# Neighbourhood attention: a unit's weighted values in one row, behind all of its copies

## The chip, the cores and the metric

One core of a Trainium2 chip runs the whole program in one launch. The metric is the device time of that core in microseconds. The engines are named as in the profile: PE (TensorE, matmuls and transpositions, with PEld for its weight loads), DVE (VectorE), ACT (ScalarE), POOL (GpSimd), SP (SyncE, which issues most DMAs).

## The reference, cut to what matters

Two blocks follow each other on 1024 tokens of width 1024. The first has a dilated attention layer and an S5 state-space layer; the second has two hybrid layers, each with a short convolution, a retention and a neighbourhood attention side by side, one output projection and a layer norm. The change concerns the neighbourhood attention (six heads of 64, a grid of 16 rows by 64 columns, a window of 8 by 16, and 256 context tokens that every query sees too) and, by a shared helper, the dilated attention.

```python
def row_block(args):
    ...
    s_loc = jnp.einsum('bhcd,bhrckd->bhcrk', q_r, k_win).astype(F32) * scale
    ...
    s_ctx = jnp.einsum('bhcd,bhjd->bhcj', q_r, kch).astype(F32) * scale
    p = jax.nn.softmax(jnp.concatenate([s_loc.reshape(b, NA_HEADS, GRID_W, n_loc), s_ctx], axis=-1), axis=-1)
    ...
    return (jnp.einsum('bhcrk,bhrckd->bhcd', p_loc, v_win)
            + jnp.einsum('bhcj,bhjd->bhcd', p_ctx, vch))
```

All of it is float32, and the kernel keeps that precision. The projections take three matmuls on rounded high and low halves (mm<-aTh,wh, mm<-aTl,wh, mm<-aTh,wl); the weighted values are plain float32 matmuls, each of which leaves two records in the trace.

## The kernel before

In a hybrid layer the neighbourhood attention goes by three pairs of heads (na_project(p), then na_core(p)). For one pair, na_core lists small functions: transpositions of the values, then units (rt, m), two halves of the grid (rt) by four column blocks (m), so 8 units for a pair, 24 for a layer and 48 in all. A unit has three steps, and step s1 of unit i, s2 of unit i-1 and s3 of unit i-2 are written together.

- **s1**: scores S of 128 queries for two heads a: 256 context keys (one PSUM tile for both heads) and 384 grid keys (a tile for each head), each product in two float32 parts. Then `soft`: DVE adds the bias and takes the maximum (L1789, L1793), and ACT takes the exponential of all 640 columns into nsb (L1796).
- **s2**: for each head four transpositions of 128 columns into a PSUM tile T (L1826), and the fifth, of the last 128 of the 640 keys, into a tile tx that both heads share (L1827). Head 0's tile is copied to nPT by DVE (L1830), head 1's by ACT (L1832), and tx to nPX by ACT (L1835). The tag T has two PSUM buffers, S three, O one; nPT has three, nPX two.
- **s3**: ten matmuls, five blocks of keys by two heads. Each puts 64 columns of V in the array and makes 64 rows of the output O; the two heads go to the two column halves. The blocks are written in the order 4, 0, 1, 2, 3, so nPX is used first, then nPT. After the last unit of a half, `put` weighs O with the gate and sends it to DRAM (yd).

The helper `together` (L128) takes these ten: it issues the first, and the others only under `issue_after(first)`, so that none comes ahead of the first. The dilated attention's s3 (L492) uses the same helper for a group of four blocks (up to 16 matmuls with V), whose copies PT are made in its s2 by DVE (L488) and ACT (L489); three other calls are in the S5 layer.

What is written around the units are projections of the next pair (mm, L168). They run `tick` now and then, which takes the next small function. The final order on each engine isn't the written one: the program is built with a scheduler that simulates a timeline and picks for each engine the ready instruction of highest priority; a priority falls with the place in the program. So the ten matmuls of a unit can come apart where something else is ready earlier.

At a layer's end, the output projection reads yd back through two slabs (ys, fetched by ACT's queue, L1974 and L1975), splits them into a high and a low half (ACT L1978, DVE L1979) and multiplies with the split output weights wo (PE L168); out_ln takes the product from PSUM (L2041).

Of the kernel before, what the change touches and what calls it, by code (L numbers as in the profile page):

```python
# [75 lines left out]
class Ker:  # L76
# [51 lines left out]
    def together(self, todo):  # L128

        mm = self.nc.tensor.matmul  # L130
        (o, w, m, a, z), *rest = todo
        first = mm(o, w, m, start=a, stop=z)  # L132
        with self.tc.issue_after(first.ins):
            for o, w, m, a, z in rest:
                mm(o, w, m, start=a, stop=z)  # L135
# [104 lines left out]
    def attn(self, zs):  # L240
# [11 lines left out]
        with ExitStack() as es:  # L252
# [194 lines left out]
            def steps(p, g, T, bt, st, O):  # L447
# [32 lines left out]
                def s2(n):  # L480
# [7 lines left out]
                    nc.vector.tensor_copy(PT[:, 0:N], t[:, 0:N])  # L488
                    nc.scalar.activation(PT[:, 256:256 + N], t[:, 256:256 + N], AF.Copy)  # L489
                    live[n] = (first, PT)  # L490

                def s3(m):  # L492

                    o = self.ps.tile([128, 512], F32, tag="O", name=self.uid("O"), bufs=1)
                    todo = []
                    for n in (4 * m + 3, 4 * m, 4 * m + 1, 4 * m + 2):
                        first, PT = live.pop(n)
# [7 lines left out]
                    self.together(todo)  # L505
# [825 lines left out]
    def hybrid(self, l, need_ctx, x_src, x_dst, xc_src=None, xc_dst=None):  # L1331
# [13 lines left out]
        with ExitStack() as es:  # L1345
# [378 lines left out]
            with ExitStack() as ns:  # L1724
# [25 lines left out]
                def na_core(p):  # L1750
# [68 lines left out]
                    def s2(rt, m):  # L1819
                        P = L.pop(("P", rt, m))  # L1820
                        out = []
                        tx = self.pt()
                        for a in range(2):
                            t = self.pt()
                            for b in range(4):
                                nc.tensor.transpose(t[:, b * 128:b * 128 + 128], P[a][:, b * 128:b * 128 + 128], self.ident)  # L1826
                            nc.tensor.transpose(tx[:, a * 128:a * 128 + 128], P[a][:, 512:640], self.ident)  # L1827
                            o = wp.tile([128, 512], F32, tag="nPT", name=self.uid("nPT"), bufs=3)
                            if a == 0:
                                V.tensor_copy(o, t)  # L1830
                            else:
                                ACT.activation(o, t, AF.Copy)  # L1832
                            out.append(o)
                        o = wp.tile([128, 256], F32, tag="nPX", name=self.uid("nPX"), bufs=2)
                        ACT.activation(o, tx[:, :256], AF.Copy)  # L1835
                        L["PT", rt, m] = (out, o)

                    def s3(rt, m):
                        PT, px = L.pop(("PT", rt, m))
# [5 lines left out]
                        for b in (4, 0, 1, 2, 3):  # L1845
                            for a in range(2):
# [4 lines left out]
                                todo.append((t, v, pp, b == 4, b == 3))  # L1851
                        self.together(todo)
# [289 lines left out]
```

## Time and profile before

| | before |
|---|---|
| median of 3 runs | 3177.37 us (3173.4 to 3179.25) |
| the profiled execution, time and span | 3182.18 us, 3180.2 us |
| PE busy | 3089.3 us, 97% |
| DVE, ACT, POOL busy | 1906.7, 1192.0, 598.4 us |
| mean granted clock of PE | 0.992 |

PE is the engine to look at. The dilated attention runs from some 350 to 1166 us, the neighbourhood units of layer 1 from 2117 to 2390 and of layer 2 from 2850 to 3081. In the profile a matmul's own duration includes the time in which the next one is already streaming, so what one costs is read from the start of one to the start of the next. Rows of equal neighbours are merged with a count.

### The profile page before, as it was taken

The page shows a single profiled execution, that of the slowest core. Times are in us where ns is not written, and L with a number is a line of the kernel's source. Part 1 is how long each engine was busy: PE and PEld are TensorE (multiplying, and loading weights), DVE is VectorE, ACT ScalarE, POOL GpSimd, SP SyncE. Part 2 cuts the span into 40 slices and gives each one's busy share as a digit, 9 for nine tenths or more (in the row PEclk, how much of TensorE's full clock was granted, in tenths as well). Part 3 has the DMA queues.
Part 4 walks back from the last instruction along what each step waited for, and adds up shares of the span by engine and source line. Part 5 has one row for each costly group of instructions (what it writes and reads, how often), then busy time and mean ns, then how long its engine had stood idle before and what let it go on. Part 6 is the DMA issues. An engine that isn't in the chain of part 4 may idle for free. (4 is left out here: it accounts for less than half of the span.)

```text
span 3180.2 us, 47784 instructions
## 1 busy us (share of the span) xinstructions
PE 3089.3 (97%) x18100; PEld 2541.0 (80%) x18100; DVE 1906.7 (60%) x4099; ACT 1192.0 (37%) x2492; POOL 598.4 (19%) x769
## 2 busy tenths in 40 slices
PE   8999999999999999999999999999999999999998
PEld 6777878777877887787878888788887888888877
DVE  4676676677666657655654634455557754465565
ACT  4222555555554544322431112244342212234351
POOL 0365120222111201111003122310002212220001
PEclk9999999999999999999999999999999999999999
DMA  5455232333233235565342211121125321121132
GB/s 199 151 184 175 68 101 82 88 108 89 82 95 88 82 103 178 172 183 158 124 145 88 80 42 59 49 81 57 48 72 161 109 67 57 57 74 58 51 118 93
DMA packets 331226, 324.05 MB, mean 102 GB/s; under 512 B 28697, under 2 KB 272116, under 8 KB 330996
## 3 DMA queue, kind: packets, MB, share of 16 engines
q1 hardware_dynamic: 322644, 312.75, 32.0%
q10 hardware_dynamic: 8352, 8.26, 0.8%
q8 instruction: 142, 2.33, 0.3%
q14 instruction: 88, 0.72, 0.1%
HBM read 248.27 MB, written 72.67 MB: 101 GB/s over the span
## 5 line engine op out<-in xcount | busy, mean ns | idle before, releaser
L168 PE MATMUL mm<-aTh,wh 128*128 128x512 f32 x2304 | 918.9, 399 | 12.4 <-ACT yr L639 3.6
L168 PE MATMUL mm<-aTl,wh 128*128 128x512 f32 x2304 | 915.8, 398 | 0.2 <-DVE aTl L1072 0.2
L168 PE MATMUL mm<-aTh,wl 128*128 128x512 f32 x2304 | 915.2, 397 | 0.6 <-DVE wl L155 0.6
L168 PEld LDWEIGHTS mm<-aTh,wh 128*128 128x128 f32 x2304 | 436.4, 189 | 104.8 <-issue 4.9
L168 PEld LDWEIGHTS mm<-aTh,wl 128*128 128x128 f32 x2304 | 435.9, 189 | 86.8 <-issue 2.4
L168 PEld LDWEIGHTS mm<-aTl,wh 128*128 128x128 f32 x2304 | 436.2, 189 | 84.7 <-issue 2.7
L155 DVE TENSOR_TENSOR wl<-wr,wh 128x1024 fp32r<-128x1024 f32 x158 | 200.3, 1268 | 209.5 <-ACT wh L154 208.2
L154 ACT ACTIVATE wh<-wr 128x1024 fp32r<-128x1024 f32 x158 | 166.9, 1057 | 336.5 <-PE mm L168 286.6
L475 ACT ACTIVATE sb<-sb,st 128x128 f32<-128x128 f32 (+1 forms) x384 | 170.1, 444 | 257.7 <-DVE st L473 256.1
L168 PE MATMUL mm<-wo,aTh 128*128 128x512 f32 x768 | 243.5, 399 | 9.8 <-DVE ys L2041 4.9
L1205 DVE SCALAR_TENSOR_TENSOR ma<-mw,cact,ma 128x256 f32<-128x256 f32 x336 | 182.9, 548 | 19.4 <-DMA mw<-in_w_mod 13.3
L168 PEld LDWEIGHTS mm<-wo,aTh 128*128 128x128 f32 x768 | 144.5, 191 | 41.7 <-DVE hs L1154 4.5
L168 PE MATMUL mm<-wo,aTl 128*128 128x512 f32 x384 | 151.8, 395 | 0.5 <-DVE aTl L1979 0.4
L473 DVE CUSTOM_DVE_ANT_0 sb<-S,bt 128x128 f32<-128x128 f32 (+1 forms) x384 | 125.0, 344 | 45.4 <-PE T L486 29.5
L427 POOL CAST qk<-kz 64x512 fp32r<-64x512 f32 x64 | 65.5, 1023 | 359.8 <-ACT kz L421 342.1
L1796 ACT ACTIVATE nsb<-nsb,nmn 128x640 f32<-128x640 f32 (+1 forms) x108 | 85.7, 793 | 99.3 <-DVE nmn L1793 84.6
L486 PE MATMUL T<-ident,sb 128*128 128x128 f32 x560 | 105.1, 284 | 13.2 <-ACT PT L489 4.1
L168 PE MATMUL mm<-vh,aTl 128*128 128x512 f32 x288 | 114.7, 398 | 0.0
L168 PE MATMUL mm<-vh,aTh 128*128 128x512 f32 x288 | 114.1, 396 | 0.0
L168 PE MATMUL mm<-vl,aTh 128*128 128x512 f32 x288 | 113.6, 395 | 0.0
L168 PE MATMUL mm<-cTh,wl 128*128 128x256 f32 x352 | 100.8, 286 | 0.6 <-DVE wl L155 0.6
L168 PE MATMUL mm<-cTh,wh 128*128 128x256 f32 x352 | 101.3, 288 | 0.0
(448 smaller groups left out, 5685.6 us busy)
## 6 DMA issues: line engine op xcount, KB each, us to landing
wr<-in_attn_w_in SPq DMA_DIRECT2D x80, 512.0 KB
wr<-in_w_in SPq DMA_DIRECT2D x64, 512.0 KB
mw<-in_w_mod SPq DMA_DIRECT2D x48, 512.0 KB
vd<-vo SPq DMA_DIRECT2D x48, 256.0 KB
Wb<-wgd SPq DMA_DIRECT2D x96, 128.0 KB
x<-x SPq DMA_DIRECT2D x24, 512.0 KB
x<-in_x SPq DMA_DIRECT2D x16, 512.0 KB
V<-vd SPq DMA_DIRECT2D x32, 256.0 KB
```

Source lines behind the costliest of these rows:

```text
L154: nc.scalar.activation(h, raw, AF.Copy)
L155: nc.vector.tensor_tensor(l, raw, h.bitcast(F32), op=ALU.subtract)
L168: nc.tensor.matmul(out, s_, m_, start=first and i == 0, stop=last and i == len(todo) - 1)
L427: nc.gpsimd.tensor_copy(at(t[o], g, hf), at(h_[r], g, hf))
L473: nc.vector.tensor_tensor_reduce(out=sb[:, :N], in0=sp[:, a * 256:a * 256 + N], in1=b, scale=1.0, scalar=3e38, op0=ALU.add, op1=ALU.min, a ...
L475: nc.scalar.activation(sb[:, :N], sb[:, :N], AF.Exp, bias=mc, scale=-1.0, accum_out=st[:, 1, g, a, n:n + 1])
L486: nc.tensor.transpose(t[:, c:c + 128], Ps[a][:, b * 128:b * 128 + 128], self.ident)
L1205: V.scalar_tensor_tensor(a, L[h][:, k], c, a, op0=ALU.mult, op1=ALU.add)
L1796: ACT.activation(sb[:, :n], sb[:, :n], AF.Exp, bias=mc, scale=-1.0, accum_out=den)
```

## The change

No instruction is added, removed or resized. Three things move.

1. `together` gets a list `made`. The first matmul waits for every instruction in it. The others are issued with a priority raised by 4000, for every caller of the helper.
2. In the neighbourhoods, the two transpositions into tx come behind the eight others (they are issued after the last of them), and all three copies go into `made`. The blocks are taken in the order 4, 3, 2, 1, 0 and the heads as 1, 0.
3. In the dilated attention the two copies of each of a group's four blocks go into `made`; the order of its matmuls stays.

```diff
@@ -125,12 +125,16 @@
         while self.bg:
             self.bg.popleft()()
 
-    def together(self, todo):
+    def together(self, todo, made=()):
+
 
         mm = self.nc.tensor.matmul
         (o, w, m, a, z), *rest = todo
         first = mm(o, w, m, start=a, stop=z)
-        with self.tc.issue_after(first.ins):
+        for i in made:
+            self.tc.add_manual_dep(first.ins, i.ins.name, mybir.DependencyInfo(
+                mybir.DependencyClass.Sync, mybir.DependencyReason.DATA), reason="together")
+        with self.tc.high_priority(4000), self.tc.issue_after(first.ins):
             for o, w, m, a, z in rest:
                 mm(o, w, m, start=a, stop=z)
 
@@ -485,16 +489,17 @@
                             c = a * 256 + b * 128
                             nc.tensor.transpose(t[:, c:c + 128], Ps[a][:, b * 128:b * 128 + 128], self.ident)
                     PT = ap.tile([128, 512], F32, tag="PT", name=self.uid("PT"), bufs=5)
-                    nc.vector.tensor_copy(PT[:, 0:N], t[:, 0:N])
-                    nc.scalar.activation(PT[:, 256:256 + N], t[:, 256:256 + N], AF.Copy)
-                    live[n] = (first, PT)
+                    made = [nc.vector.tensor_copy(PT[:, 0:N], t[:, 0:N]),
+                            nc.scalar.activation(PT[:, 256:256 + N], t[:, 256:256 + N], AF.Copy)]
+                    live[n] = (first, PT, made)
 
                 def s3(m):
 
                     o = self.ps.tile([128, 512], F32, tag="O", name=self.uid("O"), bufs=1)
-                    todo = []
+                    todo, made = [], []
                     for n in (4 * m + 3, 4 * m, 4 * m + 1, 4 * m + 2):
-                        first, PT = live.pop(n)
+                        first, PT, by = live.pop(n)
+                        made += by
                         blocks = [n] if first else [n - 1, n]
                         for b, kb in enumerate(blocks):
                             for a in (1, 0):
@@ -502,7 +507,7 @@
                                              V[:, kb, 64 * a:64 * a + 64],
                                              PT[:, a * 256 + b * 128:a * 256 + b * 128 + 128],
                                              b == 0, b == len(blocks) - 1))
-                    self.together(todo)
+                    self.together(todo, made)
                     ov = O[:, m * 512:m * 512 + 512].rearrange("p (n i) -> p n i", i=128)
                     nc.vector.tensor_copy(ov, o.rearrange("p (n i) -> p n i", i=128)[:, :, ::-1])
 
@@ -1818,38 +1823,39 @@
 
                     def s2(rt, m):
                         P = L.pop(("P", rt, m))
-                        out = []
+                        out, made = [], []
                         tx = self.pt()
                         for a in range(2):
                             t = self.pt()
                             for b in range(4):
-                                nc.tensor.transpose(t[:, b * 128:b * 128 + 128], P[a][:, b * 128:b * 128 + 128], self.ident)
-                            nc.tensor.transpose(tx[:, a * 128:a * 128 + 128], P[a][:, 512:640], self.ident)
+                                z = nc.tensor.transpose(t[:, b * 128:b * 128 + 128], P[a][:, b * 128:b * 128 + 128],
+                                                        self.ident)
                             o = wp.tile([128, 512], F32, tag="nPT", name=self.uid("nPT"), bufs=3)
-                            if a == 0:
-                                V.tensor_copy(o, t)
-                            else:
-                                ACT.activation(o, t, AF.Copy)
+                            made.append(V.tensor_copy(o, t) if a == 0 else ACT.activation(o, t, AF.Copy))
                             out.append(o)
+
                         o = wp.tile([128, 256], F32, tag="nPX", name=self.uid("nPX"), bufs=2)
-                        ACT.activation(o, tx[:, :256], AF.Copy)
-                        L["PT", rt, m] = (out, o)
+                        with self.tc.issue_after(z.ins):
+                            for a in range(2):
+                                nc.tensor.transpose(tx[:, a * 128:a * 128 + 128], P[a][:, 512:640], self.ident)
+                        made.append(ACT.activation(o, tx[:, :256], AF.Copy))
+                        L["PT", rt, m] = (out, o, made)
 
                     def s3(rt, m):
-                        PT, px = L.pop(("PT", rt, m))
+                        PT, px, made = L.pop(("PT", rt, m))
                         if m == 0:
                             L["o"] = self.ps.tile([128, 512], F32, tag="O", name=self.uid("O"), bufs=1)
                             L["sto"] = L["st"]
                         o = L["o"]
                         todo = []
-                        for b in (4, 0, 1, 2, 3):
-                            for a in range(2):
+                        for b in (4, 3, 2, 1, 0):
+                            for a in (1, 0):
                                 e = slice(a * 64, a * 64 + 64)
                                 t = o[e, m * 128:m * 128 + 128]
                                 v = Vc[:, b, e] if b < 2 else Vt[:, (rt + b - 2) * 4 + m, e]
                                 pp = PT[a][:, b * 128:b * 128 + 128] if b < 4 else px[:, a * 128:a * 128 + 128]
-                                todo.append((t, v, pp, b == 4, b == 3))
-                        self.together(todo)
+                                todo.append((t, v, pp, b == 4, b == 0))
+                        self.together(todo, made)
                         if m == 3:
                             put(o, weigh(L["sto"][:, :8].rearrange("p (m a) -> p m a", a=2),
                                          384 + p * 128, rt * 512, 4), rt)
```

How the order on PE moves is shown at three places. In each row stand the line, the operation, out<-in and the shape.

The first is the first unit of layer 1. Before, on PE (O is the output, nPX and nPT the transposed probabilities, mm a projection):

```order
L1813 MATMUL S_19557<-nk_19163,nqq_19266 128x384
L1813 MATMUL S_19557<-nkz_16703,nqq_19266 128x384
L132 MATMUL O_19595<-nPX_19545,nV_19376 64x128
L135 MATMUL O_19595<-nPX_19545,nV_19376 64x128
L135 MATMUL O_19595<-nPT_19535,nVc_19377 64x128
L168 MATMUL mm_19734<-aTh,wh_19378 128x512
L168 MATMUL mm_19734<-aTl,wh_19378 128x512
```

Seven more matmuls of this unit follow before's rows, in runs of six and one, behind eight projections. After, on PE:

```order
L172 MATMUL mm_19734<-aTl,wh_19378 128x512
L133 MATMUL O_19595<-nPX_19543,nV_19376 64x128
L139 MATMUL O_19595<-nPX_19543,nV_19376 64x128
L139 MATMUL O_19595<-nPT_19541,nV_19376 64x128
L139 MATMUL O_19595<-nPT_19534,nV_19376 64x128
L139 MATMUL O_19595<-nPT_19541,nV_19376 64x128
L139 MATMUL O_19595<-nPT_19534,nV_19376 64x128
L139 MATMUL O_19595<-nPT_19541,nVc_19377 64x128
L139 MATMUL O_19595<-nPT_19534,nVc_19377 64x128
L139 MATMUL O_19595<-nPT_19541,nVc_19377 64x128
L139 MATMUL O_19595<-nPT_19534,nVc_19377 64x128
L1818 MATMUL S_19556<-nk_19162,nqq_19265 128x384
```

The unit's ten stand in one row, with grid scores S ahead of them before and behind them now.

The second place is the end of a stretch with few projections, in layer 2. Before, on PE, the last unit of a half (T are transpositions, of the same tile nsb by L1827 into tx):

```order
L132 MATMUL O_26182<-nPX_26239,nV_25710 64x128
L135 MATMUL O_26182<-nPX_26239,nV_25710 64x128
L135 MATMUL O_26182<-nPT_26229,nVc_25711 64x128
L1826 MATMUL T_26252<-ident,nsb_26212 128x128 x4
L1827 MATMUL T_26251<-ident,nsb_26212 128x128
L135 MATMUL O_26182<-nPT_26237,nVc_25711 64x128
L135 MATMUL O_26182<-nPT_26229,nVc_25711 64x128
L135 MATMUL O_26182<-nPT_26237,nVc_25711 64x128
L135 MATMUL O_26182<-nPT_26229,nV_25710 64x128
L135 MATMUL O_26182<-nPT_26237,nV_25710 64x128
L135 MATMUL O_26182<-nPT_26229,nV_25710 64x128
L135 MATMUL O_26182<-nPT_26237,nV_25710 64x128
```

After, on PE:

```order
L1840 MATMUL T_26222<-ident,nsb_26153 128x128
L1840 MATMUL T_26222<-ident,nsb_26158 128x128
L1831 MATMUL T_26252<-ident,nsb_26212 128x128 x4
L133 MATMUL O_26182<-nPX_26237,nV_25710 64x128
L139 MATMUL O_26182<-nPX_26237,nV_25710 64x128
L139 MATMUL O_26182<-nPT_26235,nV_25710 64x128
L139 MATMUL O_26182<-nPT_26228,nV_25710 64x128
L139 MATMUL O_26182<-nPT_26235,nV_25710 64x128
L139 MATMUL O_26182<-nPT_26228,nV_25710 64x128
L139 MATMUL O_26182<-nPT_26235,nVc_25711 64x128
L139 MATMUL O_26182<-nPT_26228,nVc_25711 64x128
L139 MATMUL O_26182<-nPT_26235,nVc_25711 64x128
```

Before, a run of three and one of seven with five transpositions between; now ten, of which the last stands just behind, and the transpositions of the unit's last keys moved to a place that is four transpositions ahead of its first value.

The third is the end of layer 2's neighbourhoods. Before, on PE (wo are output weights, aTh and aTl the halves of their input):

```order
L168 MATMUL mm_28112<-wo_27969,aTh 128x512
L168 MATMUL mm_28112<-wo_27970,aTh 128x512
L168 MATMUL mm_28112<-wo_27969,aTl 128x512
L135 MATMUL O_27775<-nPT_27859,nVc_27317 64x128
L135 MATMUL O_27775<-nPT_27851,nVc_27317 64x128
L135 MATMUL O_27775<-nPT_27859,nVc_27317 64x128
L135 MATMUL O_27775<-nPT_27851,nV_27316 64x128
L135 MATMUL O_27775<-nPT_27859,nV_27316 64x128
L135 MATMUL O_27775<-nPT_27851,nV_27316 64x128
L135 MATMUL O_27775<-nPT_27859,nV_27316 64x128
L168 MATMUL mm_28138<-wo_27969,aTh 128x512
L168 MATMUL mm_28138<-wo_27970,aTh 128x512
```

After, on PE:

```order
L139 MATMUL O_27775<-nPT_27857,nVc_27317 64x128
L139 MATMUL O_27775<-nPT_27850,nVc_27317 64x128
L139 MATMUL O_27775<-nPT_27857,nVc_27317 64x128
L139 MATMUL O_27775<-nPT_27850,nVc_27317 64x128
L1873 MATMUL T_27897<-ident,non_27893 128x128 x4
L172 MATMUL mm_28112<-wo_27993,aTh 128x512
L172 MATMUL mm_28138<-wo_27993,aTh 128x512
L172 MATMUL mm_28112<-wo_27993,aTh 128x512
L172 MATMUL mm_28112<-wo_27993,aTl 128x512
L172 MATMUL mm_28112<-wo_27998,aTh 128x512
L172 MATMUL mm_28138<-wo_27993,aTh 128x512
L172 MATMUL mm_28138<-wo_27993,aTl 128x512
```

Three output matmuls stood ahead of the last run and the others behind it; now 18 of them stand ahead of this unit's first value, and behind its last come four transpositions for the gate and then the rest.

## Rows read from the trace of the kernel before

**Rows 1.** Part 1 of the page: busy us (share of span) xinstructions.

```profile
PE 3089.3 (97%) x18100; PEld 2541.0 (80%) x18100; DVE 1906.7 (60%) x4099; ACT 1192.0 (37%) x2492; POOL 598.4 (19%) x769
```

**Rows 2.** Windows, neighbourhood stretches: length, PE, PEld, DVE, ACT, POOL busy, granted clock, DMA share, GB/s.

```profile
2110.00:2190.00 80.00, 80.00 (x558) 65.51 (x557) 42.88 (x108) 39.21 (x77) 5.50 (x9) 1.00 0.19 55
2930.00:2990.00 60.00, 60.00 (x436) 49.22 (x435) 32.55 (x77) 25.14 (x54) 4.45 (x8) 1.00 0.16 46
```

**Rows 3.** PE timeline: start us, us, engine line op out<-in xcount.

```profile
2887.28 0.43 PE L132 MATMUL O<-nPX,nV 128*64 128x128 f32 x2
2887.64 0.66 PE L1826 MATMUL T<-ident,nsb 128*128 128x128 f32 x4
...
2900.47 0.39 PE L168 MATMUL mm<-aTh,wl 128*128 128x512 f32 x1
2900.69 0.39 PE L168 MATMUL mm<-aTh,wh 128*128 128x512 f32 x1
2901.01 0.32 PE L132 MATMUL O<-nPX,nV 128*64 128x128 f32 x1
...
2902.26 0.66 PE L1867 MATMUL T<-ident,non 128*128 128x128 f32 x4
...
3060.57 0.50 PE L168 MATMUL mm<-aTh,wh 128*128 128x512 f32 x1
3060.91 0.40 PE L168 MATMUL mm<-aTl,wh 128*128 128x512 f32 x1
3061.15 0.39 PE L168 MATMUL mm<-aTh,wl 128*128 128x512 f32 x1
...
3062.38 0.54 PE L135 MATMUL O<-nPT,nVc 128*64 128x128 f32 x5
...
3063.40 0.50 PE L168 MATMUL mm<-aTh,wh 128*128 128x512 f32 x1
...
3075.56 0.32 PE L132 MATMUL O<-nPX,nV 128*64 128x128 f32 x1
...
3076.14 0.66 PE L1867 MATMUL T<-ident,non 128*128 128x128 f32 x4
```

**Rows 4.** By tile and line: xcount: duration ns min/median/max, first and last start us, forms.

```profile
L1835 ACT ACTIVATE nPX<-T x48: 362/384/388, 2119.6 to 3072.9; 128x256 f32<-128x256 f32 x48
L1793 DVE CUSTOM_DVE_ANT_0 nsb<-S,tab,nmn x96: 601/618/619, 2109.7 to 3066.5; 128x384 f32<-128x384 f32 x96
L1796 ACT ACTIVATE nsb<-nsb,nmn x108: 499/830/835, 2111.3 to 3067.2; 128x640 f32<-128x640 f32 x96, 128x256 f32<-128x256 f32 x12
```

**Rows 5.** PE timeline at the end of layer 2.

```profile
3078.58 0.54 PE L135 MATMUL O<-nPT,nVc 128*64 128x128 f32 x5
...
3078.96 0.70 PE L135 MATMUL O<-nPT,nV 128*64 128x128 f32 x7
...
3090.48 0.39 PE L168 MATMUL mm<-wh,aTl 128*128 128x512 f32 x1
3093.38 0.73 PE L168 MATMUL mm<-wo,aTh 128*128 128x512 f32 x2 [2.51 <-DVE ys L2041]
```

**Rows 6.** ACT timeline of the same stretch (ACTq: its DMA issues).

```profile
3079.71 0.35 ACTq L1974 DMA_DIRECT2D ys<-yd  x1
...
3089.44 1.49 ACT L1978 ACTIVATE aTh<-ys 128x1536 fp32r<-128x1536 f32 x1 [3.44 <-DMA ys<-yd]
```

**Rows 7.** PE timeline at the end of layer 1's neighbourhoods.

```profile
2387.09 1.09 PE L1908 MATMUL O<-nPT,nVc 128*64 128x128 f32 x14
...
2394.97 1.20 PE L168 MATMUL mm<-wo,aTh 128*128 128x512 f32 x4 [1.18 <-ACT aTh L1978]
```

**Rows 8.** PE timeline, a stall in the dilated attention.

```profile
902.55 0.44 PE L486 MATMUL T<-ident,sb 128*128 128x128 f32 x2 [2.31 <-ACT PT L489]
```

**Rows 9.** Windows, columns as in group 2: a bare neighbourhood stretch, and behind that stall.

```profile
2884.30:2893.80 9.50, 9.48 (x95) 7.29 (x93) 7.42 (x19) 6.76 (x15) 2.39 (x4) 1.00 0.21 65
904.80:908.20 3.40, 3.40 (x11) 2.79 (x10) 0.86 (x7) 3.34 (x11) 0.00 (x0) 0.50 0.54 159
```

## The prediction

> **What bounds the kernel now.** I read the page's part on busy time first: TensorE (PE) is busy for 97% of the span, VectorE (DVE) for 60% [rows 1]. That is an average, so the windows of the neighbourhood stretches come next. There PE is busy for the whole of each window at a granted clock of 1.00, with DVE near half [rows 2]; in 2117 to 2390 us the table of PE's waits is empty. So in these stretches the end is set by PE alone: what PE no longer has to do shortens the kernel, unless a new wait takes it back, and a wait of any length that PE did not have before costs its full length.
>
> Then the PE timeline, for what a weighted value costs. The reader is to look at start-to-start times, because matmuls overlap and their durations don't add up. A 512-column matmul follows another after 0.22 to 0.24 us [rows 3]. The weighted values (O<-nPX, O<-nPT) are the only frequent matmuls on half the array's columns (form 128*64), and every passage from and to them costs time in which PE counts as busy. Into them: 2900.69 to 2901.01, 0.32 us where 0.22 is usual, so 0.09 to 0.10. Out of them, from the first of a run to the next other instruction: one matmul 0.36 (2887.28 to 2887.64), three 0.58 (3075.56 to 3076.14), seven 1.02 (3062.38 to 3063.40), ten 1.25 (2901.01 to 2902.26). The two heads run as a pair, a further pair costs 0.22, and an odd run costs as much as the next even one. And the matmul behind an exit is late for its own successor: 3060.57 to 3060.91 is 0.34, the next step 0.24, so 0.10 more [rows 3].
>
> **Part 1, whole units (the gain).** Nothing is removed; there are 48 units of ten weighted matmuls in both kernels, the last run of them starting at 3078.58 [rows 5]. In before's order they stand in 111 runs: 12 of one, 17 of two, 33 of three, 1 of four, 5 of five, 3 of six, 36 of seven, 2 of eight, 2 of ten. In after's order all 48 are runs of ten. With the prices above (two 0.37, four 0.59, five 0.80, six 0.81, eight 1.03) the 111 runs cost 12x0.36 + 17x0.37 + 33x0.58 + 0.59 + 5x0.80 + 3x0.81 + 36x1.02 + 2x1.03 + 2x1.25 = 78.1 us, plus 111 entries of 0.09, 10.0: 88.1. The 48 whole ones cost 48x(1.25+0.09) = 64.3. Difference 23.8. The late successors add 63 fewer times 0 to 0.10: 0 to 6.3. Together 24 to 30. Walking the same prices over the 111 runs in the timeline one by one, with the true neighbours of each, I get 99.7 us before and 67 to 69 after, so 30 to 33. I take **-30**, where both meet, since nearly every exit has a follower that shows the excess, and keep 24 and 33 for the range. All of it is on the path [rows 2].
>
> The Trainium skill (TensorEngine Tiling (Array Packing), Key Properties) says that changing the tiling mode drains TensorE, without a price; TensorE: Matmul & The Clock Gate, Single matmul latency, puts the constant part of an isolated matmul at 398/2.4, 166 ns. Two drains of that size for each of 63 passages would be an estimate of 21 us, and the sum below would end 9 us later, near 3164. The rows show more, because an odd run also wastes half a pair.
>
> **Part 2, the same helper elsewhere.** In the attention the runs fall from 51 to 48 (three blocks were cut in two), in the SSM one 64-row group is no longer cut. Four passages at 0.25 to 0.5 us: **-1** to -2. There the first matmul now waits for eight copies; it belongs to the block that is made last (4m+3) in both kernels, and its own copy was already among those, so the wait adds at most the other engine's half, and nothing behind it in the order needs less. I cost it at nothing; the cover is the projection filler that stands between. But the whole PE order of the attention shifts by some rows, and PE does stall there now and then. One such stall, 2.31 us at 902.55, is followed by a window at half clock, 0.50 for 3.4 us, which loses another 1.7 [rows 8, 9]. One stall more or fewer is 4 us: I take **0**, with 4 either way.
>
> **Part 3, the waits on copies (the loss).** A unit's first value now needs nPX, the last copy (ScalarE, ACT, L1835, 0.38 us), and this stands behind the transpositions that were moved to the unit's end. The instruction that waits heads PE's queue, so everything behind it waits too: projection filler, the next scores, and by them DVE's and ACT's softmax. Where filler stands between, it covers: 0.38 us is two 512-column steps. In order, some 40 of the 48 units have that. In about eight, in bare stretches with few or no projections, the first value follows the last transposition by 0.2 to 1.5 us of PE work. Price of one: the copy needs some 0.7 us from the last transposition's start, and longer if an exponential (0.83) or nPT stands ahead in ACT's queue [rows 4]; so 0 to 0.9 us of stall each, below 8x0.9 = 7. The same bare stretches also bring the scores nearer to their own transpositions: the chain of bias (0.62) and exponential (0.83) is 1.45 us without the reads of their sums [rows 4], and after has stretches with 2.4 to 3.8 us of PE work for it and for the second head's, where before had 3.4 and more. Walking one of them (its last rows are the second place shown with the change) gives 2.5 us for it all. Two to four such stretches: 2 to 10. I take **+4**, nearest to two walked stretches with something to spare; the lower bound is 0, since the windows show no wait at all for a softmax as it stands now [rows 2], and no gain is possible from a wait that is not there.
>
> **Part 4, the tails.** At the end of layer 2 the last run of weighted values starts at 3078.58; its output frees the pool that a fetch on ACT's queue needs (issue 3079.71), then come the splits (ACT's at 3089.44 for 1.49, DVE's behind it) and the third output tile's matmul at 3093.38, after PE idled 2.51 [rows 5, 6]. That chain, 13.7 us from the run's end at 3079.66, keeps its length. Before, 45 output matmuls (10.2 us, the last at 3090.48) cover it; after, 15 of them stand ahead of the last run, so 30 and four transpositions are left, some 7.3. The wait grows by 3. **+3** (0 if the fetch gets out earlier, 6 if a half clock follows a 5.5 us wait; the 2.51 here was followed by none). At the end of layer 1 the context values (2387.09) close the pass and PE waits 1.18 at 2394.97 for a split [rows 7]; after, 18 output matmuls move ahead of them and the chain behind is as long, with one weight split later: **+1.5** (0 to 4).
>
> **Sum.** -30 - 1 + 0 + 4 + 3 + 1.5 = -22.5. Against the profiled run (3182.18, of which 3180.2 is span) that is 3159.7; this run lies 4.8 above the median of 3177.37, so the forecast for the median is **3155**.
>
> **Rivals.** *Cover holds everywhere* (no new waits): -31 alone, 3146. For it: DVE and ACT have half their time free [rows 2]. Against it: the two tails are chains that already wait [rows 5 to 7]. *Waits take half back without touching the clock*: all eight thin units at 0.9, four stretches at 2.5, both tails at their upper ends, 6 and 4: -31 + 7 + 10 + 10 = -4, 3173; with half of that beyond the forecast, 3164. *Slower*: the bare stretches. There are twelve half passes (two per head pair, three pairs, two layers), each with a place where filler runs out. If PE waits there as at 902.55, 2.31 us, and the clock then drops as it did after it, each costs 4.0 us [rows 8, 9]; with the tails' 4.5 the gain of 31 is used up at seven of them, and it is slower by over 6.4 from nine; at twelve the time is 3199. For it: that pairing of stall and half clock stands in the trace. Against it: in the bare stretch of before, where the same work stands, PE kept busy at a clock of 1.00 [rows 9], and the walked stall is spread over several places well below 2 us. *The change does not do what it says*: it could be that a run is still cut, or that a run's passages cost nothing once neighbours change; the order shows 48 whole runs, so only the second is left, and then the sum is the waits alone, +8, 3186.
>
> **Chances.** Forecast 0.58 (3148 to 3163), cover holds 0.15, half taken back 0.16 (3163 to 3173), slower by the bare stretches 0.06, passages free 0.05. The range reaches from 3141 (33 gained, a stall fewer in the attention, no wait) to 3172. A difference of 0.2%, 6.4 us, is about what a measurement of this kernel tells from none: faster is below 3171.0, slower above 3183.7. The first two cases and three quarters of the third are faster; what is left of it and half of the passages case is the same: faster 0.85, same 0.07, slower 0.08.
>
> **What would show it.** Right: 48 runs of ten in the PE timeline, 1.25 us from first value to the next other instruction, PE's busy time down by about 31 us, its idle time up by some 8, of which a wait of 5 to 6 us for DVE's ys near the end of layer 2, one of 2 to 3 behind the context values, and short ones for nPX (L1835) and nsb (L1796) in bare stretches. Wrong: busy time down by 21 or less (then passages cost less than the rows say), waits on nPX in units with filler, or windows of the neighbourhood stretches with a clock under 1.00.

## The result and the profile after

The changed kernel took 3161.56 us (median of 4 runs, 3156.46 to 3164.38) against 3178.23 for the kernel before (4 runs): a ratio of 0.9947, 95% interval 0.9935 to 0.9959. That is 16.7 us less; 3155 with a range of 3141 to 3172 was predicted. The profiled run took 3164.38 us, 3162.6 of them span, so the pair of traces differs by 17.6 us in span.

Part 1 of the page of the changed kernel, which answers to [rows 1]:

```profile
span 3162.6 us, 47833 instructions
PE 3061.4 (97%) x18100; PEld 2540.3 (80%) x18100; DVE 1894.9 (60%) x4099; ACT 1189.5 (38%) x2492; POOL 605.0 (19%) x769
```

PE is busy for 27.9 us less, and it idles for 10.3 us more (101.2 against 90.9). A unit in the PE timeline of the changed kernel, to be held against the pieces of [rows 3] (start us, us, then the instruction):

```profile
2126.25 0.93 PE L1831 MATMUL T<-ident,nsb 128*128 128x128 f32 x7
2127.11 0.32 PE L133 MATMUL O<-nPX,nV 128*64 128x128 f32 x1
...
2127.38 0.61 PE L139 MATMUL O<-nPT,nV 128*64 128x128 f32 x8
2127.82 0.61 PE L139 MATMUL O<-nPT,nVc 128*64 128x128 f32 x8
2128.35 0.39 PE L1818 MATMUL S<-nk,nqq 128*128 128x256 f32 x1
2128.58 0.28 PE L1818 MATMUL S<-nkz,nqq 128*128 128x256 f32 x1
2128.70 0.29 PE L1818 MATMUL S<-nk,nqq 128*128 128x256 f32 x1
```

From the first value to the score behind the unit it is 1.24 us, the score's successor is late by 0.11 (0.23 where the next step is 0.12), and in all 48 units the first value and the next other instruction are 1.24 us apart. Walked one by one as in the prediction (start-to-start times, entry and late successor included) they cost 69.3 us, of which 0.7 is PE waiting at their ends; the 111 runs before cost 99.7.

To see where the rest went I cut both traces at the same places of the program. The first two windows of each kernel end with the attention's last weighted value and with the first score of a neighbourhood; the third is the two hybrid layers from there to the last matmul. Of the kernel before, then of the changed one (length, PE busy and so on, the granted clock third from the end):

```profile
0.00:1165.10 1165.10, 1118.42 (x6418) 907.10 (x6420) 777.17 (x2065) 557.84 (x1385) 280.04 (x362) 0.99 0.37 113
1165.10:2098.60 933.50, 911.85 (x5232) 759.50 (x5229) 513.26 (x804) 267.80 (x465) 160.74 (x223) 0.99 0.37 115
2098.60:3170.60 1072.00, 1058.65 (x6454) 874.37 (x6453) 612.18 (x1225) 365.09 (x640) 155.81 (x181) 1.00 0.25 79
```

```profile
0.00:1157.10 1157.10, 1113.26 (x6420) 913.71 (x6420) 771.50 (x2065) 557.70 (x1385) 280.83 (x362) 0.99 0.38 113
1157.10:2090.10 933.00, 910.28 (x5231) 757.79 (x5227) 513.79 (x804) 267.79 (x465) 162.15 (x223) 0.99 0.37 115
2090.10:3152.60 1062.50, 1037.45 (x6454) 868.80 (x6454) 605.47 (x1225) 362.77 (x640) 160.21 (x181) 0.99 0.26 80
```

So the attention's part is 8.0 us shorter, which was not expected, and the hybrid layers are only 9.5 shorter, where the forecast's terms for them come to 21.5. In the layers PE is busy for 21.2 us less and idles for 25.05 instead of 13.35 us. What it waits for there, of the changed kernel (engine and line, what it waited for, us in total, times, longest):

```profile
PE mm L172 <- DVE ys L2047: 7.5, 3, 4.9
PE mm L172 <- ACT wo L158: 4.8, 2, 2.8
PE mm L172 <- ACT ch L1393: 2.8, 1, 2.8
PE mm L172 <- DVE wo L159: 2.8, 3, 1.2
PE T L1831 <- ACT nPT L1834: 2.1, 4, 0.7
...
PE O L133 <- ACT nPX L1841: 0.5, 1, 0.5
```

Before, the weights (wo) and the copies (nPT, nPX) are not in this table, and ys and ch read:

```profile
PE mm L168 <- DVE ys L2041: 4.9, 2, 2.5
PE T L215 <- DVE ys L2056: 3.1, 1, 3.1
PE mm L168 <- ACT ch L1388: 1.4, 1, 1.4
```

So the waits for ys are no longer in sum (8.0 us in two rows before, 7.5 now); the new ones are those for weights and copies, and 1.4 us more for ch.

The ends of the layers in PE's timeline, layer 2 first, are what to set beside [rows 5] and [rows 7]:

```profile
3060.07 0.66 PE L1873 MATMUL T<-ident,non 128*128 128x128 f32 x4
3063.52 1.22 PE L172 MATMUL mm<-wo,aTh 128*128 128x512 f32 x2 [2.79 <-ACT wo L158]
3065.57 0.79 PE L172 MATMUL mm<-wo,aTh 128*128 128x512 f32 x1 [0.83 <-DVE wo L159]
3066.16 0.63 PE L172 MATMUL mm<-wo,aTl 128*128 128x512 f32 x1
...
2373.77 1.09 PE L1914 MATMUL O<-nPT,nVc 128*64 128x128 f32 x14
2376.89 0.82 PE L172 MATMUL mm<-wo,aTh 128*128 128x512 f32 x2 [2.03 <-ACT wo L158]
2378.87 0.79 PE L172 MATMUL mm<-wo,aTh 128*128 128x512 f32 x1 [1.16 <-DVE wo L159]
...
2392.91 1.22 PE L172 MATMUL mm<-wo,aTh 128*128 128x512 f32 x2 [4.88 <-DVE ys L2047]
```

In layer 2 four transpositions stand behind the last value, in layer 1 none, and the next output matmul waits for a weight that isn't split yet. Two windows of the changed kernel show what follows these stalls (columns as above):

```profile
3063.50:3070.30 6.80, 5.95 (x13) 4.26 (x14) 5.22 (x7) 3.07 (x4) 0.00 (x0) 0.50 0.80 282
2377.40:2384.20 6.80, 5.64 (x14) 4.17 (x14) 4.11 (x5) 1.75 (x3) 0.95 (x1) 0.50 1.03 389
```

Half clock: a 512-column matmul takes 0.43 us there and not 0.23. Over the whole span the mean granted clock fell from 0.992 to 0.988; the trace has two levels, 1.0 and 0.5, with 75 us at the lower one instead of 53, so some 11 us of PE time more. Of the 22 us, 13.7 lie in the attention's window and 10.2 in the layers; between them it is 3.4 less.

The layers' 9.5 us then add up like this: some 31 us less for the runs, 11.7 more idle time, 5.1 more by half clock, and 4.6 more of other PE work, whose cause these traces don't show.

### The profile page after: what moved, and what is told of

Read it like the earlier page. It is cut to its first block, busy times and chain, and to the rows that moved or that the text cites. A ratio compares the mean times of both kernels' runs of the same rounds, so it can differ in the third digit from the quotient of the medians.

```text
span 3162.6 us, 47833 instructions
## 1 busy us (share of the span) xinstructions
PE 3061.4 (97%) x18100; PEld 2540.3 (80%) x18100; DVE 1894.9 (60%) x4099; ACT 1189.5 (38%) x2492; POOL 605.0 (19%) x769
## 5 line engine op out<-in xcount | busy, mean ns | idle before, releaser
L172 PE MATMUL mm<-aTh,wh 128*128 128x512 f32 x2304 | 917.2, 398 | 16.7 <-ACT yr L644 3.7
```

What stands on the lines that cost most here:

```text
L172: nc.tensor.matmul(out, s_, m_, start=first and i == 0, stop=last and i == len(todo) - 1)
```

## The experiments

Each of the ten kernels was timed beside the kernel before on the same chip; ratios are to that. These theories stood against each other at first. **A**: every passage between array tilings has its price, wherever it is, and the time follows their number and the waits. **Rivals**: the gain of the first part is chance (B), the wait on the copies decides (D), half-cut units gain nothing (E).

### The neighbourhoods alone, the attention alone

In `together`, the attention's calls and the S5 layer's get the old helper:

```diff
+        if not made:
+            with self.tc.issue_after(first.ins):
+                for o, w, m, a, z in rest:
+                    mm(o, w, m, start=a, stop=z)
+            return
         with self.tc.high_priority(4000), self.tc.issue_after(first.ins):
...
-                    self.together(todo, made)
+                    self.together(todo)
```

> The changed kernel with the dilated attention and the SSM left as before: the helper waits and raises priorities only for the neighbourhoods. Its order has 48 whole units of ten there, and in the attention the 51 runs of before. Theory A (each passage between array tilings costs its price, wherever it is): the walked price of the units' runs is 69 us as in the changed kernel (99.7 before), PE's waits in the two hybrid layers are about 25 us as there, and the time up to the first neighbourhood scores is that of before (2098.6 us) again, some 8 more than in the changed kernel (2090.1). So about 3168 us (3164 to 3173). Rival B (the 8 us of the first 1166 us were a chance of the clock's half-speed windows and not of the helper's use there): then this kernel is as fast as the changed one, 3158 to 3164.

Measured: 3169.0 us, ratio 0.9975 (0.9965 to 0.9984). The first neighbourhood score starts at 2096.4 us, the layers take 1066.2 with 30 us of idle time, the runs' price is 69 us.

The other half leaves the neighbourhoods' s2 and s3 and their helper as before, and keeps wait and priority in the attention (and the priority in the S5 layer):

```diff
+        if na:
+            with self.tc.issue_after(first.ins):
+                for o, w, m, a, z in rest:
+                    mm(o, w, m, start=a, stop=z)
+            return
         for i in made:
...
-                        self.together(todo, made)
+                        self.together(todo, na=True)
```

> Before with the helper's wait and raised priority in the dilated attention and the SSM only; the neighbourhoods keep steps, block order and helper of before. Its order has 48 runs of weighted values in the attention instead of 51, 641 instead of 661 borders between transpositions and other matmuls ahead of the neighbourhoods, and the neighbourhood runs of before (111). Theory A: the first 2098 us shrink by some 8 us as in the changed kernel, the rest stays, so 3170 us (3166 to 3174), and the walked price of the neighbourhood runs is 99 to 100 us. Rival B: nothing of that, 3175 to 3181.

Measured: 3171.65 us, ratio 0.9981 (0.9972 to 0.999). The three windows of this kernel:

```profile
0.00:1163.10 1163.10, 1117.80 (x6420) 916.53 (x6420) 775.64 (x2065) 557.66 (x1385) 279.46 (x362) 0.98 0.38 113
1163.10:2091.40 928.30, 907.71 (x5233) 755.77 (x5229) 513.44 (x804) 267.74 (x465) 161.70 (x223) 1.00 0.37 115
2091.40:3162.80 1071.40, 1058.50 (x6454) 874.00 (x6453) 614.95 (x1225) 364.80 (x640) 154.38 (x181) 1.00 0.26 79
```

The layers are those of before (1071.4, PE busy 1058.5), and the first 2091.4 us are 7 shorter. But 5 of these 7 lie behind the attention, where this trace has 6.8 us at half clock and before 17.1, so one trace's lengths say little here. The timed runs say more: without the helper's use there the ratio is 0.9975 instead of 0.9947, and with it alone 0.9981. So B falls: it is worth some 6 us (0.0019), a third of the whole result, although it joins only three cut runs. All the traces agree: in the seven kernels with wait and priority in the attention, its last value starts between 1155.8 and 1163.1 us (mean 1159.1), in the two with the priority alone at 1162.1 and 1164.6, in the three without either between 1165.1 and 1168.8 (mean 1166.8). PE's busy time up to there, less half of the time at half clock, is 1096.4 to 1100.6 us in the nine with the raised priority and 1108.5 to 1109.1 in the three without, so this gain comes with the priority, and it is not the clock's.

### The priority alone, the order alone

Without the loop that adds the waits:

```diff
-        for i in made:
-            self.tc.add_manual_dep(first.ins, i.ins.name, mybir.DependencyInfo(
-                mybir.DependencyClass.Sync, mybir.DependencyReason.DATA), reason="together")
```

> The changed kernel without the first value's wait for the copies; the raised priority and the new order of transpositions and blocks stay. Its order has 46 whole units and two in two pieces (2 and 8). Theory A: price of the runs about 70 us, time as the changed kernel within 3 us, 3158 to 3165, since the wait changes the order at two units only. Rival D (the wait is what makes a unit whole or what costs the new idle time in the bare stretches): then this kernel has some 4 us less idle time in the neighbourhood stretches and ends near 3156, or the two cut units come with stalls inside and it ends above 3166.

Measured: 3164.92 us, ratio 0.9946 (0.9931 to 0.9962), the changed kernel's own. With the new order of the transpositions the wait on the copies does nothing that can be measured, so D falls in both its forms.

With neither wait nor priority, s2 and s3 of the changed kernel alone:

```diff
-        with self.tc.high_priority(4000), self.tc.issue_after(first.ins):
+        with self.tc.issue_after(first.ins):
```

> Before with one part of the change alone: the last keys' transpositions close a unit, blocks are taken 4, 3, 2, 1, 0 with the heads 1, 0. The helper is that of before, with no wait on copies and no raised priority. Its order has the neighbourhood units in 82 runs (23 of ten) instead of 111 (2 of ten). Theory A: by the prices of the prediction (0.36 for one to 1.25 for ten from the first value to the next other instruction, and 0.19 for entry and late successor) the runs cost 83 us instead of 99.7, so 16 less; the waits at the layers' ends are smaller than in the changed kernel because the last values come as early as before: 3164 to 3168. Rival E (only whole units gain, a half-cut one gives it back by waits): 3172 to 3179.

Measured: 3187.5 us, ratio 1.0021 (1.0012 to 1.003): slower than before, and both expectations missed. The runs did become cheaper, by 17 us in the trace, as theory A's prices had it (16); its waits failed. But from the first score to the last matmul it is 1078.6 us against 1072.0, with 29.7 us of idle time instead of 13.3:

```profile
PE mm L169 <- DVE ys L2044: 12.0, 3, 5.7
PE mm L169 <- DVE wo L156: 3.7, 3, 1.8
PE T L1828 <- ACT nPT L1831: 3.1, 3, 1.7
PE mm L169 <- ACT ch L1390: 2.8, 1, 2.8
PE O L133 <- ACT nPX L1838: 1.9, 1, 1.9
PE mm L169 <- ACT wo L155: 1.7, 1, 1.7
```

These are the changed kernel's new waits, with 17 of its 31 us of cheaper runs and without the attention's gain. In both orders 18 output-weight matmuls stand ahead of the last values of each layer; before, it is none in layer 1 and 3 in layer 2. That gave a new theory, **F**: the helper makes the gain, and the closing transpositions (those of the last keys, now behind the unit's eight others) make the waits. Its rival **G**: the ends wait for weights and fetches that come at their own pace, so any time saved ahead of them is waited for.

### The helper with the steps of before

s2 and s3 keep the inline transpositions and the blocks 4, 0, 1, 2, 3 of before; the copies still go into `made`. Against the changed kernel:

```diff
-                        with self.tc.issue_after(z.ins):
-                            for a in range(2):
-                                nc.tensor.transpose(tx[:, a * 128:a * 128 + 128], P[a][:, 512:640], self.ident)
...
+                            nc.tensor.transpose(tx[:, a * 128:a * 128 + 128], P[a][:, 512:640], self.ident)
                             o = wp.tile([128, 512], F32, tag="nPT", name=self.uid("nPT"), bufs=3)
...
-                        for b in (4, 3, 2, 1, 0):
-                            for a in (1, 0):
+                        for b in (4, 0, 1, 2, 3):
+                            for a in range(2):
```

> The changed kernel with the neighbourhood steps of before: the last keys' transpositions stand behind each head's four again, blocks are taken 4, 0, 1, 2, 3; the helper's wait on all copies and its raised priority stay, in the attention too. Its order has the same 48 whole units of ten, but no output-weight matmul ahead of layer 1's last value and 3 ahead of layer 2's, as before (the changed kernel has 18 and 18). Theory F (the price of passages is gained by the helper alone, and the new waits at the layers' ends come from the closing transpositions, which let 18 output matmuls past the last values): from the start of the neighbourhoods to the last matmul 1072 - 28 us for the runs, 0 to 4 for bare stretches, PE idle there below 18 us (before 13.3, changed 25.1), and the first part as in the changed kernel: 3141 to 3149 us. Rival G (the ends wait for weights, fetches and splits that come at their own pace, so whatever PE saves ahead of them is waited for): idle 25 us or more, 3156 to 3164.

Measured: 3141.14 us (4 runs, 3138.05 to 3144.3), ratio 0.9884 (0.9869 to 0.9898): 36 us faster than before, and well ahead of the changed kernel (0.9947). Its layers and its waits there:

```profile
2085.00:3130.20 1045.20, 1028.39 (x6454) 867.07 (x6453) 609.75 (x1225) 363.67 (x640) 156.36 (x181) 0.99 0.26 82
```

```profile
PE T L219 <- DVE ys L2061: 5.2, 1, 5.2
PE mm L172 <- ACT ch L1393: 2.8, 1, 2.8
PE mm L172 <- DVE ys L2046: 2.8, 3, 2.3
PE mm L172 <- ACT aTh L1983: 1.8, 1, 1.8
...
PE T L1832 <- ACT nPT L1837: 0.6, 1, 0.6
```

The waits for wo are gone, and idle time is 16.8 us. G falls. This kernel and the one with the attention alone differ only in the helper's use in the neighbourhoods: 1071.4 to 1045.2 us, PE busy 30.1 less, idle 3.9 more. By the walk the runs are 32 us cheaper, and 3.4 us more at half clock take 1.7 back: this is the cleanest reading of 111 against 48 runs, though the rest of the layers' order moves with it.

### The two steps one by one

First the changed kernel with the blocks and heads in the order of before, then with the transpositions in the place of before (of the diff above, the second half alone, and the first half alone).

> The changed kernel with the blocks in the order of before (4, 0, 1, 2, 3, heads 0, 1); the last keys' transpositions still close a unit. 48 whole units, 18 output-weight matmuls ahead of the last values in both layers. Theory F: as the changed kernel, 3157 to 3165, PE idle from the neighbourhoods to the last matmul 23 to 30 us. Rival G: the same. If the order of blocks were what costs, it would end below 3152.

> The changed kernel with the last keys' transpositions in the place of before, and the changed order of blocks (4, 3, 2, 1, 0, heads 1, 0). 48 whole units; none and 10 output-weight matmuls ahead of the last values. Theory F: idle between before's 13 and 20 us, 3142 to 3151. Rival G: 3156 to 3164.

Measured: 3166.7 us (1.7 above F's range), ratio 0.9964 (0.9952 to 0.9976), with 27.5 us of idle time in the layers; and 3146.25 us, ratio 0.9898 (0.9883 to 0.9914), with 18.5. So it is the closing transpositions that cost. The order of the blocks is worth nothing that these runs can tell for sure.

The steps of before with the raised priority, but no wait on the copies (the loop above taken out):

> As old_order, but without the first value's wait for the copies: raised priority alone, with the steps of before. Its order has 23 whole units of ten and most others cut into 3 and 7; none and 18 output-weight matmuls ahead of the last values. Theory A with F: some 23 runs more than old_order at 0.40 and 0.15 us each, 12 to 13 us of PE time, and the waits of the end of layer 2 as in the changed kernel, 3 to 8 us: 3157 to 3168. Rival: the cut costs nothing where the neighbours are transpositions, within 4 us of old_order.

Measured: 3165.29 us, ratio 0.9955 (0.994 to 0.9969). The runs cost 12.3 us more than with the wait (85.2 against 72.9, the context's six pieces included in both), as theory A expected, so the rival falls. PE idles 17.9 us in the layers, and the end of layer 2 waits 3.8 us for wo. The wait on the copies is what makes a unit whole as long as the last keys' transpositions stand inside it: the first three values (nPX twice, head 0's nPT) are ready ahead of head 1's nPT. Its worth is 23 us here (0.0071 of ratio; 16 us of it in the layers, 1061.3 against 1045.2, the rest ahead of them, where the attention lost the wait too) and nothing that can be measured with closing transpositions: the change does the same thing twice, and the second way is the dear one.

### The layers' ends or every unit

The step of the closing transpositions is made conditional on the head pair:

```diff
+                            if not (p == 2):
+                                nc.tensor.transpose(tx[:, a * 128:a * 128 + 128], P[a][:, 512:640], self.ident)
...
+                        if p == 2:
+                            with self.tc.issue_after(z.ins):
```

> As old_order (helper with wait and priority, blocks as before), but in the last head pair of each layer, 16 of 48 units, the last keys' transpositions close a unit as in the changed kernel. 48 whole units; 18 output-weight matmuls ahead of the last values in both layers again. Theory F (the closing transpositions cost at the layers' ends alone, by the output matmuls that they let past): nearly the whole difference between tx_last (3166.7) and old_order (3141.1) comes back, 3155 to 3167, PE idle from the neighbourhoods to the last matmul 22 to 29 us (old_order 16.8). Rival H (they cost in every unit, by a later copy): a third of the difference, 3147 to 3152.

> As old_order, but in the first two head pairs of each layer, 32 of 48 units, the last keys' transpositions close a unit; in the last pair they stand in the place of before. 48 whole units; none and 3 output-weight matmuls ahead of the last values, as in old_order. Theory F: as old_order within 4 us, 3138 to 3146, idle 15 to 20 us. Rival H: two thirds of the difference, 3154 to 3160.

The second has `p < 2` for `p == 2`. Measured: 3161.19 us, ratio 0.9936 (0.9922 to 0.995), and 3155.1 us, ratio 0.9923 (0.9909 to 0.9936). Against 0.9884 without any, the last pair's 16 units cost 0.0052 (16 us) and the other 32 cost 0.0039 (12 us). Each of these differences is uncertain by some 6 us; in the traces the layers are 13.1 and 8.9 us longer, 22.0 together, and with all units closing 21.7. So F holds for the ends, where a third of the units makes more than half of the loss, but it missed the second kernel by 9 us: H is right that the others pay. In the last pair's kernel the waits for the ends are back:

```profile
PE mm L172 <- DVE ys L2050: 9.1, 3, 6.0
PE mm L172 <- ACT wo L158: 3.6, 3, 2.8
PE mm L172 <- DVE wo L159: 2.8, 3, 1.6
```

In the other kernel they are not; there PE's transpositions wait for nPT instead:

```profile
PE T L219 <- DVE ys L2065: 4.5, 1, 4.5
PE T L1831 <- ACT nPT L1836: 3.4, 5, 0.8
PE mm L172 <- ACT ch L1393: 2.8, 1, 2.8
```

The layers of that kernel are 8.9 us longer than with the steps of before (1054.1 against 1045.2): 2.9 of that is idle time, 3.4 us more at half clock are 1.7, and PE's other work is 4 longer. The trace shows a small part of the last, some 1 us: values next to scores instead of transpositions (a run of values begins or ends at a score in 26 places against 6), and behind an exit a score is late for its successor by 0.105 us where a transposition is by 0.057. Where the other 3 to 4 us come from is not shown.

All of them side by side; "layers" is the time from the first neighbourhood score to the last matmul in the trace, "idle" PE's idle time in it, "half" its time at half clock, "runs" the walked price of all half-column runs of the neighbourhoods, the context's six included and waits left out, and "rest" what is left of the difference from before when idle time, runs and half of the time at half clock are taken off:

| kernel | ratio | layers | idle | half | runs | rest |
|---|---|---|---|---|---|---|
| before | 1 | 1072.0 | 13.3 | 10.2 | 105.0 | 0 |
| changed | 0.9947 | 1062.5 | 25.1 | 20.5 | 74.0 | 4.6 |
| neighbourhoods alone | 0.9975 | 1066.2 | 30.2 | 17.1 | 73.9 | 4.9 |
| attention alone | 0.9981 | 1071.4 | 12.9 | 10.2 | 105.0 | -0.1 |
| priority alone | 0.9946 | 1066.4 | 28.4 | 20.5 | 74.7 | 4.4 |
| order alone | 1.0021 | 1078.6 | 29.7 | 17.1 | 87.7 | 4.1 |
| steps of before | 0.9884 | 1045.2 | 16.8 | 13.7 | 72.9 | 0.1 |
| closing transpositions | 0.9964 | 1066.9 | 27.5 | 27.3 | 74.3 | 2.8 |
| new order of blocks | 0.9898 | 1048.7 | 18.5 | 17.1 | 73.0 | -0.1 |
| steps of before, no wait | 0.9955 | 1061.3 | 17.9 | 17.1 | 85.2 | 1.0 |
| last pair closing | 0.9936 | 1058.3 | 23.5 | 23.9 | 73.5 | 0.9 |
| first two pairs closing | 0.9923 | 1054.1 | 19.8 | 17.1 | 73.6 | 3.6 |

The rest is 3 to 5 us wherever the transpositions close the units of the first two pairs, and at most 1 elsewhere. So closing transpositions cost PE work too, and not only waits; through what is open.

## Why the prediction was right, and where its steps failed

The time lies in the range and 6.6 us above the forecast. The terms were less good than their sum: the attention gave 7 us more than its term, the ends took 7 more than theirs, and 4.6 us of other PE work had no term. That errors of this size nearly cancel is luck; the first and largest term is not.

**Part 1, whole units: right.** -30 was forecast, 99.7 to 69.3 is -30.4 in the traces, and attention alone and steps of before, which differ in the helper's use in the neighbourhoods alone, have 30.1 us of PE time between them. The choice of the walked price over the lower end was right. Two of the Trainium skill's constants for an isolated matmul (TensorE: Matmul & The Clock Gate, Single matmul latency) for each of 63 passages would have made it an estimate of 21 us; the measurement decides against it here.

**Part 2, the attention: mis-sized.** -1 with 4 either way was forecast; the attention's part is 8.0 us shorter in the traces and the kernel with it alone 6 faster. The step that failed was to count only cut runs. The raised priority reorders transpositions, scores and projections too: 20 borders fewer between transpositions and others ahead of the neighbourhoods (641 against 661), and at full clock PE needs 8 to 13 us less for the same matmuls up to the attention's last value (idle time and half clock taken out, all kernels with the raised priority against all without). Which of these moves saves it is not shown. At the same time more of that part runs at half clock, 34.1 us against 20.5 in the changed kernel.

**Part 3, the copies: right in sum, wrong in the wait.** +4 was forecast, and idle time between first and last value of the two layers is 5.1 us, 0.8 of it for a weight. But of the two waits that the sum was made from, the one for nPX is 0.5 us in all, once, and the one for the softmax (nsb) 0.3. Most of the rest is transpositions (L1831) that wait for nPT's copy by ACT, 2.1 us in four places. The tag T has two PSUM buffers, and tx, taken first and copied last in both kernels, holds one of them; that its later copy is why the next transpositions wait is argued from the code, not tried. The prediction had not asked what the moved step keeps occupied.

**Part 4, the ends: the mis-sized term.** +4.5 was forecast. From the last values on, idle time rose by 5.2 us behind layer 1 and 1.5 behind layer 2, 1.4 of the first at ch, and 10.2 us more at half clock followed, 5 us of PE time: some 12. The prediction saw that 15 to 18 output matmuls move ahead of the last values and that a chain would be bare. It named the wrong chain in layer 2 (the fetch of ys; it was the weights: the split of wo stands on ACT right behind another one, of wh, which waits for a load that arrives at 3061.4) and allowed for no half clock, since the one stall of 2.51 us in [rows 5] was followed by none. ACT and SP in the changed kernel at that place:

```profile
3061.47 1.06 ACT L158 ACTIVATE wh<-wr 128x1024 fp32r<-128x1024 f32 x1 [2.69 <-DMA wr<-in_w_out]
3062.43 2.94 ACT L158 ACTIVATE wo<-wr 128x1024 fp32r<-128x1024 f32 x3
...
3055.43 0.33 SPq L152 DMA_DIRECT2D wr<-in_w_out  x1
```

That load was issued 4.6 us ahead of the transpositions that follow the last value, and PE had nothing left to do until wo was split behind it. That the 15 matmuls which now stand ahead filled this time before is read from the order; in steps of before, where they stand behind the last values again, the waits for wo are gone.

**The rivals.** That the bare stretches bring the loss did not happen; from each layer's first unit to its last value the clock stays at 1.00. Of the other side the right mechanism was there (a stall, then half clock), but at the layers' ends, and too small to turn the sign. With the order alone, where 17 us of cheaper runs stand against 16.4 us of new idle time, 3.4 by half clock and 4.1 of the rest, the sign does turn: 1.0021.

## What to carry to other kernels

When one instruction group is to stay whole, give it one means and see which of its parts does the work: here the wait on all copies and the raised priority alone are worth 36 us, and a third step with the same aim takes 20 of them back. A step that is moved later moves what follows it past the end of its stage; look there for the work that used to cover the next stage's loads. And price passages between array tilings from start-to-start times, since they count as busy time and stand in no table of waits; leave waits at their ends out, or they are counted twice.

## What the runs showed of the hardware

A transposition that stands next to a half-column run is a cheaper neighbour than a full matmul: it is late for its own successor by 0.057 us, the matmul by 0.105, and the way in is 0.09 from either. And part of the spread between equal runs goes with the time at half clock: the changed kernel's four runs have mean clocks of 0.988, 0.988, 0.99 and 0.99 at 3164.4, 3163.8, 3159.3 and 3156.5 us. It isn't all of it: of neighbourhoods alone, two runs at 0.992 took 3164.0 and 3174.6 us.
